# The order of wide and narrow matmul passes in a seven-product scheme, and one weight split earlier

## The chip, the core and the metric

The kernel runs on one core of one Trainium2 chip. The metric is device time in microseconds (us) from start to end of one execution; lower is better. On the core, TensorE (PE) multiplies a stationary block of 128x128 weights with a moving block of up to 512 columns and adds the result into a bank of PSUM (128 partitions x 512 floats). ScalarE (ACT), VectorE (DVE) and GpSimd (POOL) do element-wise work, SyncE (SP) issues most DMA transfers. Each engine works through its own list in order and waits on semaphores of the others.

## What is computed

A decoder trunk of two layers on 512 tokens of width 1024 (tokens are the columns, channels the partitions, 8 chunks of 128). Layer 0 mixes tokens by a gated linear recurrence and pooled differences, layer 1 by a convolution module; each then has cross-attention into 256 memory tokens and a gated feed-forward block (FFN) with a short convolution. The two parts that matter here:

```python
def conformer_conv(x, norm, w1, b1, dw_w, dw_b, ln_g, ln_b, w2, b2):
    h = rms_norm(x, norm) @ w1 + b1
    h = jax.nn.glu(h, axis=-1)
    h = causal_dwconv(h, dw_w, dw_b)
    h = jax.nn.silu(layer_norm(h, ln_g, ln_b))
    return h @ w2 + b2

def conv_ffn(x, norm, w_up, dw_w, dw_b, w_down):
    h = rms_norm(x, norm) @ w_up
    g = causal_dwconv(h[..., :D_FF], dw_w, dw_b)
    u = h[..., D_FF:]
    return (jax.nn.gelu(g) * u) @ w_down
```

with D_FF = 3072.

## The kernel before

**Split operands.** Every float32 operand is split into a high part (`hi`, rounded by a ScalarE copy) and a low part (`lo = x - hi`, a VectorE subtraction). A product is then high x high + high x low + low x high, three matmul passes for each 128 channels of the contraction (`mm3`, lines 187 to 192: L190, L191, L192 are the three passes). Weights come by DMA into a buffer `raw` (a ring of 3) and are split by `load_w` into `whi` and `wlo` (L170 on ScalarE, L171 on VectorE).

**Seven products.** The FFN's up projection computes two channel blocks (gate and value, 128 channels each) from two halves of the contraction and two halves of the tokens. It uses a scheme with seven block products instead of eight, with sums of weight blocks ("s1" to "s4") and sums of token halves (T1 to T4); "a11", "a12", "a22" are plain blocks. Each product runs over 4 chunks of 128 channels and 256 tokens. For channels 6 to 21 (`WIDE`) the high and the low part of the tokens lie side by side in one tile of 512 columns, so that a chunk takes two passes: a *wide* one of 512 columns (high weights times [high | low]) and a *narrow* one of 256 columns (low weights times high, added into the left half of the bank). `Seven.product` (line 812) writes them, L820 is the matmul:

```python
steps = [(ps, wh, x), (ps[:, :M], wl, x[:, :M])]
for i, (to, part, by) in enumerate(steps if c < 3 else steps[::-1]):
```

So one product is the series wide, narrow, wide, narrow, wide, narrow, narrow, wide. For the other channels a product takes the three passes of `mm3`, each of 256 columns.

**A unit.** `unit(c)` of `ffn` is one channel's turn. On TensorE, in a row: s1 (into the bank `stat`, called H), s2 (into F), a12 (into G), s3 (into F), then the down projection of an earlier channel (24 passes of 512 columns, `mm3`), then a11 of the next channel (`ahead`), s4 (into H) and a22 (into F). Between them ScalarE and VectorE empty the banks (L175, L958, L970 and others), split the weight blocks of the coming channel (L862 high, L869 low), and GpSimd's DMA queue forms the weight sums. The FFN and the attention stand in `manual_schedule` regions: there the program order of each engine is the order written in the code. `mm_ps()` gives the next bank of a pool of 5 (`mm`) or, at every few calls while `wide[0]` is set, of a pool of 2 (`aux`); `stat_ps()` gives the one bank `stat`.

**The end of the convolution module** (layer 1, lines 1750 to 1820). After the layer norm the eight chunks `outs[c]` are multiplied by the norm's scale (`scaled`, L1778, VectorE), passed through SiLU (`silu`, L1782, ScalarE) and split (L180 high, L185 low) to `xs[c]`. At the same time the memory values of layer 1 end: their sums (L468, TensorE) stand in the banks `ps[0]` and `ps[1]`, and `mem.scaled` takes them out (L474 on ScalarE, L478 on VectorE), which sets the banks free. The eight output projections `pw2` follow in the order `PAIRED` = 0, 4, 1, 5, ...: the first three together, chunk by chunk as `xs[c]` gets ready (`project_all`), the others one after the other (`project`). Behind the manual region a list scheduler orders the instructions.

Of the kernel before, what the change touches and what calls it, by code (L numbers as in the profile page):

```python
# [15 lines left out]
P = 128  # L16
T = 512
# [4 lines left out]
M = 256  # L22
# [8 lines left out]
PAIRED = (0, 4, 1, 5, 2, 6, 3, 7)  # L31
# [31 lines left out]
def trunk(ctx: ExitStack, tc: tile.TileContext, I: dict, out: list):  # L63
    nc = tc.nc
    V, A, G, PE = nc.vector, nc.scalar, nc.gpsimd, nc.tensor
# [14 lines left out]
    def nm(s):  # L80
        uid[0] += 1
        return f"{s}_{uid[0]}"
# [16 lines left out]
    def main_ps():  # L99
        return psum.tile([P, T], F32, tag="mm", name=nm("mm"))  # L100

    def aux_ps():
        return aux.tile([P, T], F32, tag="aux", name=nm("aux"))
# [3 lines left out]
    def mm_ps():  # L107

        wide[1] += 1
        return aux_ps() if wide[0] and wide[1] % 7 in (2, 5) else main_ps()  # L110

    def stat_ps():
        return stat.tile([P, T], F32, tag="stat", name=nm("stat"))
# [37 lines left out]
    def load_w(src=None, eng=None, raw=None, parts=1, ahead=AHEAD, park=False):  # L151

        with tc.high_priority(ahead):
            if raw is None:
                raw = wp.tile([P, D], F32, tag="raw", name=nm("raw"), bufs=3)
                fetched[0] = nc.sync.dma_start(raw, src)
            if park:
                both = [split(raw[:, i : i + T], None, None, eng) for i in (0, T)]
                return [b[0] for b in both], [b[1] for b in both]
            hi = wp.tile([P, D], F32R, tag="whi", name=nm("whi"))  # L160
            lo = wp.tile([P, D], F32R, tag="wlo", name=nm("wlo"))
            n = D // parts
            for i in range(0, D, n):
                split(raw[:, i : i + n], hi[:, i : i + n], lo[:, i : i + n], eng)
        return hi, lo

    def split(src, hi=None, lo=None, eng=None):
        hi = act_r() if hi is None else hi
        lo = act_r() if lo is None else lo
        A.activation(hi, src, AF.Copy)  # L170
        fetched[1] = (eng or V).tensor_tensor(lo, src, hi.bitcast(F32), op=ALU.subtract)  # L171
        return hi, lo
# [5 lines left out]
    def high(src, hi=None):  # L178
        hi = act_r() if hi is None else hi
        A.activation(hi, src, AF.Copy)  # L180
        return hi

    def low(src, hi, lo=None):
        lo = act_r() if lo is None else lo
        V.tensor_tensor(lo, src, hi.bitcast(F32), op=ALU.subtract)  # L185
        return hi, lo

    def mm3(ps, w, x, first, last, onto=False):
        (wh, wl), (xh, xl) = w, x
        PE.matmul(ps, wh, xh, start=first, stop=False, skip_group_check=onto)  # L190
        PE.matmul(ps, wh, xl, start=False, stop=False, skip_group_check=onto)  # L191
        return PE.matmul(ps, wl, xh, start=False, stop=last, skip_group_check=onto)  # L192
# [16 lines left out]
    def blk(w, i, n=P):  # L209
        hi, lo = (w.hi, w.lo) if isinstance(w, Piece) else w  # L210
        if isinstance(hi, list):
            hi, lo, i = hi[i // T], lo[i // T], i % T
        return hi[:, i : i + n], lo[:, i : i + n]
# [158 lines left out]
    def project_all(ws, xs, ps=None, at=0, last=True):  # L372

        ps = ps or [mm_ps() for _ in ws]
        for k, x in enumerate(xs, at):
            for w, p in zip(ws, ps):
                mm3(p, blk(w, k * P), x, k == 0, last and k == C - 1)
        return ps
# [361 lines left out]
    class Seven:  # L740
# [68 lines left out]
                    move(hi[:, M:], lo[:, :M])  # L809
            self.beside.add(j)  # L810

        def product(self, ps, w, j, first=True):

            for c in range(4):
                wh, wl = blk(w, c * P)
                if ps.shape[-1] == T:
                    x = self.both(j, c)
                    steps = [(ps, wh, x), (ps[:, :M], wl, x[:, :M])]
                    for i, (to, part, by) in enumerate(steps if c < 3 else steps[::-1]):
                        PE.matmul(  # L820
                            to, part, by, start=first and c == 0 and i == 0, stop=c == 3 and i == 1, skip_group_check=True
                        )
                else:
                    mm3(ps, (wh, wl), self.block(j, c), first and c == 0, c == 3, not first)
            return ps

    class Blocks:
# [51 lines left out]
    def pairs_of(layer):  # L879
        return {c: Blocks(I["wpair"][layer * (CF - PLAIN) + c - PLAIN]) for c in range(PLAIN, CF)}  # L880

    def ffn(layer, norm, nxt, seven, pairs):
# [105 lines left out]
            V.tensor_tensor(ys[c][1], y, ys[c][0].bitcast(F32), op=ALU.subtract)  # L988

        def m(c, ps, block, j, first=True):  # L990
            seven.product(ps, pairs[c].w[block], j, first)

        def ahead(c):

            G, F = bank(c), bank(c)
            m(c, G, "a11", seven.B11)
            if c == WIDE[0] + 1:
                PE.matmul(F, pairs[c].w["a11"][0][:, :P], seven.both(seven.B11, 0), start=True, stop=True)
            A.activation(F, G, AF.Copy)
            return G, F  # L1000

        def unit(c):
# [3 lines left out]
            down, seeded = downs.get(c), c > GC  # L1006
            H = stat_ps() if wide(c) else main_ps()[:, :M]
            m(c, H, "s1", seven.T1)
            if c <= second:
                high(c + 1, "s3")  # L1010
            next(left, None)
            if c <= second:
                low(c + 1, "s3")

            m(c, F, "s2", seven.T2, False)
            u, f, g = tmp_f(), tmp_f(), tmp_f()
            if wide(c):
# [167 lines left out]
        first, second = PLAIN, PLAIN + 1  # L1185
        done.update((first, name) for name in ("a11", "a22", "a12", "s3", "s1", "s2"))
        with tc.high_priority(AHEAD):
            w = [Piece(I["wup"][(layer * 2 + k) * PLAIN]) for k in range(2)]
# [9 lines left out]
        if nxt:  # L1198
# [10 lines left out]
            for j in range(C // 2):  # L1209
                for i in range(2):  # L1210
                    ps = mm_ps()
# [314 lines left out]
    def conformer(norm, nxt, mem, parked):  # L1526
# [136 lines left out]
        xs = [None] * C  # L1663
        mem.eng = G
        with tc.manual_schedule(engines=ORDERED | {mybir.EngineType.SP}):
            key2 = mem.products(parked[2], ks=range(4))
            ps0, (xh, xl) = [mm_ps(), mm_ps()], norm.x[0]
            first = [(p, blk(ws[k], 0)) for p, k in zip(ps0, ("G0", "V0"))]
# [56 lines left out]
            ps = [[mm_ps(), mm_ps()] for _ in range(2)]  # L1725
            mem.eng = None
            steps = (_ for h in range(2) for _ in mem.sums(h, ps[h], ready[4 * h :]))
# [24 lines left out]
            def halves(raw):  # L1752
                both = [split(raw[:, i : i + T]) for i in (0, T)]
                return [b[0] for b in both], [b[1] for b in both]

            pw = [halves(raws[0])]
# [19 lines left out]
            def scaled(c):  # L1776
                if c < C:
                    V.tensor_tensor(outs[c], outs[c], r, op=ALU.mult)  # L1778

            def silu(c):  # L1780
                if c < C:
                    A.activation(outs[c], outs[c], AF.Silu, scale=col("c_ln_g", c), bias=col("c_ln_b", c))  # L1782
# [4 lines left out]
            for c in range(C):  # L1787
                hi = high(outs[c])
                silu(c + 1)
                scaled(c + 2)  # L1790
                xs[c] = low(outs[c], hi)
                if c == 0:
                    mem.scaled(0, ps[0])
                elif c == 1:
                    pw.append(load_w(I["pw2"][PAIRED[2]]))
                elif c == 5:
                    mem.scaled(1, ps[1])
            mem.eng = None
# [3 lines left out]
        def finish(n, ps):  # L1802
            V.scalar_tensor_tensor(X[n], ps, col("c_b_pw2", n), X[n], op0=ALU.add, op1=ALU.add)
            nxt.feed(n)

        six = Seven(nxt, 3)
        for n, ps in zip(PAIRED, project_all(pw, xs)):
            finish(n, ps)
        for n in PAIRED[3:]:
            if n == 5:  # L1810
# [13 lines left out]
    with tc.manual_schedule(engines=ORDERED | {mybir.EngineType.SP}):  # L1824
# [20 lines left out]
        ps = [[mm_ps(), mm_ps()] for _ in range(2)]  # L1845
        steps = mem.sums(0, ps[0], ready)
# [19 lines left out]
        steps = mem.sums(1, ps[1], late)  # L1866
# [7 lines left out]
        w = [Piece(I["wk"][0])]  # L1874
# [55 lines left out]
    pairs = pairs_of(0)  # L1930
    mem, parked = ffn(0, n2, n3, attention(0, n1, mem, n2, six, pairs[PLAIN]), pairs)
    six = conformer(n3, n4, mem, parked)
    pairs = pairs_of(1)
    ffn(1, n5, None, attention(1, n4, mem, n5, six, pairs[PLAIN]), pairs)
# [78 lines left out]
```

## Time and profile before

| | us |
|---|---|
| median of 3 runs | 1421.2 (1420.17 to 1423.81) |
| the profiled execution | 1420.88 |
| its span, first to last instruction | 1419.1 |
| TensorE busy | 1408.8 |
| VectorE busy | 1139.4 |
| ScalarE busy | 938.0 |
| GpSimd busy | 318.1 |

The granted TensorE clock is 0.999 of full speed over the span. A row of the timeline reads: start, duration (both us from the span's start), engine, source line, operation, the tile written and the tiles read, partitions x columns, count of merged instructions, and in brackets the engine's idle time before it and what ended that. TensorE's matmuls are pipelined, so a row's duration overlaps the next row; the distance of two starts tells what a pass took. A row of the waits reads: who waited, for whom, us in total, times, the longest. In the rows of "order" below, which come from the program and have no times, a matmul reads bank<-moving operand,weights.

### The profile page before, as it was taken

How to read it: one execution, taken by the hardware profiler on the slowest of the kernel's cores; microseconds unless marked ns; L12 is line 12 of the kernel's file. 1: busy time of each engine (PE TensorE's matmuls, PEld its weight loads, DVE VectorE, ACT ScalarE, POOL GpSimd, SP SyncE). 2: the span in 40 equal slices, each digit the busy share in tenths (PEclk: the TensorE clock that was granted, in tenths of full speed). 3: DMA queues.
4: the chain of work that ended last, by engine and by line, in shares of the span. 5: the costliest groups of instructions: out<-in, count | busy, mean ns of one | idle time of the engine just before them, and what ended most of it. 6: DMA issues, size and time to landing. Idle time of an engine off the chain costs nothing.

```text
span 1419.1 us, 21330 instructions
## 1 busy us (share of the span) xinstructions
PE 1408.8 (99%) x7756; PEld 1214.8 (86%) x7756; DVE 1139.4 (80%) x1924; ACT 938.0 (66%) x1688; POOL 318.1 (22%) x333
## 2 busy tenths in 40 slices
PE   9999999999999999999999999999999999999998
PEld 7988888998898888888988777899889888888897
DVE  6987776778877888878799997968788788788775
ACT  7678744776567676676666547766756766766664
POOL 0011310110122222222008993011002222222211
PEclk9999999999999999999999999999999999999999
DMA  8623232544387777676433454345338776776751
GB/s 300 202 75 102 92 119 82 112 119 131 99 204 168 165 178 177 162 179 170 123 119 119 119 158 154 105 89 137 107 98 194 180 175 163 177 178 162 169 135 60
DMA packets 80026, 204.23 MB, mean 144 GB/s; under 512 B 9008, under 2 KB 9520, under 8 KB 79920
## 3 DMA queue, kind: packets, MB, share of 16 engines
q1 hardware_dynamic: 50688, 149.89, 32.7%
q0 software_dynamic: 28800, 52.44, 21.5%
q8 instruction: 61, 1.00, 0.3%
q10 hardware_dynamic: 432, 0.54, 0.1%
q14 instruction: 45, 0.37, 0.1%
HBM read 145.16 MB, written 2.10 MB: 104 GB/s over the span
## 4 chain that ended last, share of the span: by engine, by line
PE 92%; DVE 2%; ACT 2%; DMA 2%; issue 1%; POOL 0%; SPq 0%; ACTq 0%; DVEq 0%; POOLq 0%
PE mm L820 16%; PE mm L190 15%; PE mm L192 15%; PE mm L191 15%; PE aux L190 7%; PE aux L191 7%; PE aux L192 7%; PE stat L820 6%; PE mm L468 1%; PE mm L1571 1%; DVE wlo L171 1%; DMA raw<-in_wk 1%; DMA raw<-in_wv 1%; ACT whi L170 1%; PE aux L542 0%
## 5 line engine op out<-in xcount | busy, mean ns | idle before, releaser
L190 PE MATMUL mm<-act,whi 128*128 128x512 f32 (+2 forms) x803 | 295.8, 370 | 0.6 <-ACT whi L170 0.5
L191 PE MATMUL mm<-act,whi 128*128 128x512 f32 (+2 forms) x803 | 295.7, 368 | 0.1
L192 PE MATMUL mm<-act,wlo 128*128 128x512 f32 (+2 forms) x803 | 295.6, 368 | 0.0
L190 PEld LDWEIGHTS mm<-act,whi 128*128 128x128 f32 x803 | 151.1, 188 | 26.9 <-ACT whi L170 0.9
L191 PEld LDWEIGHTS mm<-act,whi 128*128 128x128 f32 x803 | 151.3, 188 | 25.5 <-DVE act L171 1.0
L192 PEld LDWEIGHTS mm<-act,wlo 128*128 128x128 f32 x803 | 151.3, 188 | 25.1 <-DVE wlo L171 0.6
L869 DVE TENSOR_TENSOR bigr<-raw,bigr 128x512 fp32r<-128x512 f32 x176 | 120.4, 686 | 64.0 <-ACT bigr L862 63.4
L862 ACT ACTIVATE bigr<-raw 128x512 fp32r<-128x512 f32 x176 | 109.4, 622 | 83.3 <-DVE wlo L207 80.8
L190 PE MATMUL aux<-act,whi 128*128 128x512 f32 x399 | 155.5, 390 | 0.0
L191 PE MATMUL aux<-act,whi 128*128 128x512 f32 x399 | 155.3, 389 | 0.0
L192 PE MATMUL aux<-act,wlo 128*128 128x512 f32 x399 | 155.2, 389 | 0.0
L875 POOL DMA_DIRECT2D raw<-wa x100 | 96.4, 983 | 254.1 <-DVE bigr L869 167.2
L820 PE MATMUL mm<-bigr,bigr 128*128 128x512 f32 (+1 forms) x768 | 150.9, 339 | 0.0
L170 ACT ACTIVATE whi<-raw 128x1024 fp32r<-128x1024 f32 (+1 forms) x95 | 96.5, 1020 | 81.9 <-PE mm L191 44.1
L820 PEld LDWEIGHTS mm<-bigr,bigr 128*128 128x128 f32 x768 | 124.4, 188 | 17.5
L872 POOL DMA_DIRECT2D raw<-raw x50 | 43.3, 866 | 385.8 <-DVE wlo L869 304.1
L171 DVE TENSOR_TENSOR wlo<-raw,whi 128x1024 fp32r<-128x1024 f32 (+1 forms) x75 | 90.2, 1210 | 18.2 <-ACT whi L170 17.9
L820 PE MATMUL mm<-act,whi 128*128 128x512 f32 x256 | 95.6, 397 | 0.0
L192 PEld LDWEIGHTS aux<-act,wlo 128*128 128x128 f32 x399 | 74.9, 188 | 15.8
L191 PEld LDWEIGHTS aux<-act,whi 128*128 128x128 f32 x399 | 75.0, 188 | 15.6
L877 POOL DMA_DIRECT2D raw<-wa x50 | 43.2, 864 | 200.3 <-DVE bigr L869 94.2
L190 PEld LDWEIGHTS aux<-act,whi 128*128 128x128 f32 x399 | 74.9, 188 | 14.1
(377 smaller groups left out, 3391.5 us busy)
## 6 DMA issues: line engine op xcount, KB each, us to landing
raw<-wa POOLq DMA_DIRECT2D x150, 256.0 KB, 3.9
wa<-in_wpair SPq DMA_DIRECT2D x88, 256.0 KB, 3.7
raw<-in_wpair SPq DMA_DIRECT2D x44, 512.0 KB, 4.0
big<-in_wdown SPq DMA_DIRECT2D x42, 512.0 KB, 4.6
raw<-raw POOLq DMA_DIRECT2D x50, 256.0 KB, 3.8
raw<-in_pw SPq DMA_DIRECT2D x24, 512.0 KB, 3.8
raw<-in_win SPq DMA_DIRECT2D x20, 512.0 KB, 3.5
raw<-in_wk SPq DMA_DIRECT2D x16, 512.0 KB, 3.6
```

The source lines that it names most:

```text
L170: A.activation(hi, src, AF.Copy)
L171: fetched[1] = (eng or V).tensor_tensor(lo, src, hi.bitcast(F32), op=ALU.subtract)
L190: PE.matmul(ps, wh, xh, start=first, stop=False, skip_group_check=onto)
L191: PE.matmul(ps, wh, xl, start=False, stop=False, skip_group_check=onto)
L192: return PE.matmul(ps, wl, xh, start=False, stop=last, skip_group_check=onto)
L468: PE.matmul(p, m[j], x, start=k == 0 and j == 0 and x is hi, stop=k == C - 1 and x is lo)
L820: PE.matmul(to, part, by, start=first and c == 0 and i == 0, stop=c == 3 and i == 1, skip_group_check=True)
L862: A.activation(self.w[name][0], self.block(name), AF.Copy)
L869: V.tensor_tensor(lo, self.block(name), hi.bitcast(F32), op=ALU.subtract)
L872: G.dma_start(self.r, self.z, accum_op=ALU.add)
L875: G.dma_start(block, self.a22, accum_op=ALU.add)
L877: G.dma_start(self.r, self.a12, accum_op=ALU.add)
```

## The change

In wide products the four wide passes stand together and the four narrow ones together. A product is *plain* (wide first) or *turned* (narrow first); turned are s4, a22, s2 and s3 in the FFN. At the end of the convolution module the load and split of the third `pw2` weight moves from the second turn of the loop over chunks to the first, and `mem.scaled(0)`, the values' scaling, from the first to the second; the third projection's bank is `stat` instead of the next of `mm_ps()`.

```diff
-        def product(self, ps, w, j, first=True):
-
-            for c in range(4):
-                wh, wl = blk(w, c * P)
-                if ps.shape[-1] == T:
-                    x = self.both(j, c)
-                    steps = [(ps, wh, x), (ps[:, :M], wl, x[:, :M])]
-                    for i, (to, part, by) in enumerate(steps if c < 3 else steps[::-1]):
-                        PE.matmul(
-                            to, part, by, start=first and c == 0 and i == 0, stop=c == 3 and i == 1, skip_group_check=True
-                        )
-                else:
-                    mm3(ps, (wh, wl), self.block(j, c), first and c == 0, c == 3, not first)
+        def product(self, ps, w, j, first=True, turned=False):
+
+            blocks = [(blk(w, c * P), self.both(j, c) if ps.shape[-1] == T else self.block(j, c)) for c in range(4)]
+            if ps.shape[-1] == T:
+                steps = [(ps, wh, x) for (wh, _), x in blocks], [(ps[:, :M], wl, x[:, :M]) for (_, wl), x in blocks]
+                steps = steps[1] + steps[0] if turned else steps[0] + steps[1]
+                for i, (to, part, x) in enumerate(steps):
+                    PE.matmul(to, part, x, start=first and i == 0, stop=i == 7, skip_group_check=True)
+            else:
+                for c, (part, x) in enumerate(blocks):
+                    mm3(ps, part, x, first and c == 0, c == 3, not first)
             return ps
...
         def m(c, ps, block, j, first=True):
-            seven.product(ps, pairs[c].w[block], j, first)
+            seven.product(ps, pairs[c].w[block], j, first, block in ("s4", "a22", "s2", "s3"))
...
                 if c == 0:
+                    pw.append(load_w(I["pw2"][PAIRED[2]]))
+                elif c == 1:
                     mem.scaled(0, ps[0])
-                elif c == 1:
-                    pw.append(load_w(I["pw2"][PAIRED[2]]))
                 elif c == 5:
                     mem.scaled(1, ps[1])
...
-        for n, ps in zip(PAIRED, project_all(pw, xs)):
+        for n, ps in zip(PAIRED, project_all(pw, xs, [mm_ps(), mm_ps(), stat_ps()])):
             finish(n, ps)
```

TensorE, the products s1 (bank `stat_4402`) and s2 (bank `mm_4359`) of the first wide channel of layer 0, before: s1 and the first two rows of s2.

```order
L820 MATMUL stat_4402<-bigr_3236,bigr_4350 128x512
L820 MATMUL stat_4402<-bigr_3236,bigr_4350 128x256
L820 MATMUL stat_4402<-bigr_3236,bigr_4350 128x512
L820 MATMUL stat_4402<-bigr_3236,bigr_4350 128x256
L820 MATMUL stat_4402<-bigr_3237,bigr_4350 128x512
L820 MATMUL stat_4402<-bigr_3237,bigr_4350 128x256 x2
L820 MATMUL stat_4402<-bigr_3237,bigr_4350 128x512
L820 MATMUL mm_4359<-bigr_3238,bigr_4353 128x512
L820 MATMUL mm_4359<-bigr_3238,bigr_4353 128x256
```

The same place after the change: s1, which is plain, and the whole of s2, which is turned.

```order
L819 MATMUL stat_4402<-bigr_3236,bigr_4350 128x512 x2
L819 MATMUL stat_4402<-bigr_3237,bigr_4350 128x512 x2
L819 MATMUL stat_4402<-bigr_3236,bigr_4350 128x256 x2
L819 MATMUL stat_4402<-bigr_3237,bigr_4350 128x256 x2
L819 MATMUL mm_4359<-bigr_3238,bigr_4353 128x256 x2
L819 MATMUL mm_4359<-bigr_3239,bigr_4353 128x256 x2
L819 MATMUL mm_4359<-bigr_3238,bigr_4353 128x512 x2
L819 MATMUL mm_4359<-bigr_3239,bigr_4353 128x512 x2
```

The same sixteen passes; the eight narrow ones of two products now stand in one row.

TensorE at the first three `pw2` projections, before. `mm_8965`, `mm_8966` and `mm_8967` are their banks; `act_8898` and `act_8902` are high and low part of chunk 0, `act_8908` and `act_8912` of chunk 1; `whi_8916` and `wlo_8917` are the third weight.

```order
L190 MATMUL mm_8965<-act_8898,act_8808 128x512
L191 MATMUL mm_8965<-act_8902,act_8808 128x512
L192 MATMUL mm_8965<-act_8898,act_8809 128x512
L190 MATMUL mm_8966<-act_8898,act_8854 128x512
L191 MATMUL mm_8966<-act_8902,act_8854 128x512
L192 MATMUL mm_8966<-act_8898,act_8855 128x512
L190 MATMUL mm_8965<-act_8908,act_8808 128x512
L190 MATMUL mm_8966<-act_8908,act_8854 128x512
L190 MATMUL mm_8967<-act_8898,whi_8916 128x512
L191 MATMUL mm_8967<-act_8902,whi_8916 128x512
L191 MATMUL mm_8965<-act_8912,act_8808 128x512
```

After: `whi_8906` and `wlo_8907` are the third weight, `stat_8967` its bank, `act_8910` and `act_8914` are chunk 1.

```order
L190 MATMUL mm_8965<-act_8898,act_8808 128x512
L191 MATMUL mm_8965<-act_8902,act_8808 128x512
L192 MATMUL mm_8965<-act_8898,act_8809 128x512
L190 MATMUL stat_8967<-act_8898,whi_8906 128x512
L191 MATMUL stat_8967<-act_8902,whi_8906 128x512
L190 MATMUL mm_8965<-act_8910,act_8808 128x512
L192 MATMUL stat_8967<-act_8898,wlo_8907 128x512
L190 MATMUL stat_8967<-act_8910,whi_8906 128x512
L191 MATMUL mm_8965<-act_8914,act_8808 128x512
L192 MATMUL mm_8965<-act_8910,act_8809 128x512
L191 MATMUL stat_8967<-act_8914,whi_8906 128x512
L192 MATMUL stat_8967<-act_8910,wlo_8907 128x512
```

The third projection has changed places with the second (`mm_8966`), whose passes on chunks 0 and 1 now follow as a block of six.

VectorE at the same place, before (`bigr<-mm` are the scaled values, `actf` the chunks):

```order
L1778 TENSOR_TENSOR actf_7910<-actf_7910,aux_8874 128x512
L185 TENSOR_TENSOR act_8902<-actf_7682,act_8898 128x512
L478 SCALAR_TENSOR_TENSOR bigr_7204<-mm_8702,rt,bigr_7203 128x512
L478 SCALAR_TENSOR_TENSOR bigr_7206<-mm_8703,rt,bigr_7205 128x512
L1778 TENSOR_TENSOR actf_8019<-actf_8019,aux_8874 128x512
L185 TENSOR_TENSOR act_8912<-actf_7779,act_8908 128x512
L171 TENSOR_TENSOR wlo_8917<-raw_8914,whi_8916 128x1024
```

And after:

```order
L1776 TENSOR_TENSOR actf_7910<-actf_7910,aux_8874 128x512
L185 TENSOR_TENSOR act_8902<-actf_7682,act_8898 128x512
L171 TENSOR_TENSOR wlo_8907<-raw_8904,whi_8906 128x1024
L1776 TENSOR_TENSOR actf_8019<-actf_8019,aux_8874 128x512
L185 TENSOR_TENSOR act_8914<-actf_7779,act_8910 128x512
L478 SCALAR_TENSOR_TENSOR bigr_7204<-mm_8702,rt,bigr_7203 128x512
L478 SCALAR_TENSOR_TENSOR bigr_7206<-mm_8703,rt,bigr_7205 128x512
```

The third weight's low half now stands ahead of chunk 1's low half, and the two steps that free the banks `mm_8702` and `mm_8703` behind it. ScalarE's list moves in the same way: `whi_8906` stands where the first two L474 stood.

## The prediction

> **What bounds the kernel now.** I read the page first, then the waits of TensorE, then the order of its passes in time.
>
> ```profile
> span 1419.1 us, 21330 instructions
> PE 1408.8 (99%) x7756; PEld 1214.8 (86%) x7756; DVE 1139.4 (80%) x1924; ACT 938.0 (66%) x1688; POOL 318.1 (22%) x333
> PE 92%; DVE 2%; ACT 2%; DMA 2%; issue 1%; POOL 0%; SPq 0%; ACTq 0%; DVEq 0%; POOLq 0%
> PE stat L143 <- POOL onesf L132: 1.0, 1, 1.0
> PE mm L468 <- ACT whi L170: 0.9, 1, 0.9
> PE mm L190 <- ACT whi L170: 0.5, 1, 0.5
> ```
>
> TensorE (PE) is busy 99% and carries 92% of the chain; its three longest waits are 1.0, 0.9 and 0.5 us. So the kernel ends when PE has started its last pass, and an edit is worth what it takes off the distances from one pass's start to the next. A matmul's row says it lasts 0.40 (512 columns) or 0.28 us (256), but the next one starts well before that end; only starts count. One product of the feed-forward blocks (a11 of one channel), and the start of the next:
>
> ```profile
> 601.45 0.40 PE L820 MATMUL mm<-act,whi 128*128 128x512 f32 x1
> 601.68 0.28 PE L820 MATMUL mm<-act,wlo 128*128 128x256 f32 x1
> 601.80 0.40 PE L820 MATMUL mm<-act,whi 128*128 128x512 f32 x1
> 602.03 0.28 PE L820 MATMUL mm<-act,wlo 128*128 128x256 f32 x1
> 602.15 0.40 PE L820 MATMUL mm<-act,whi 128*128 128x512 f32 x1
> 602.39 0.40 PE L820 MATMUL mm<-act,wlo 128*128 128x256 f32 x2
> 602.63 0.40 PE L820 MATMUL mm<-act,whi 128*128 128x512 f32 x1
> 602.87 1.58 PE L820 MATMUL mm<-bigr,bigr 128*128 128x512 f32 x8
> ```
>
> Four wide passes (W) and four narrow ones (N) take 602.87 - 601.45 = 1.42 us. What they would take without changes of width is read where many of one kind stand together, in the cross-attention: 24 wide, 24 narrow, 24 wide.
>
> ```profile
> 307.19 0.28 PE L190 MATMUL aux<-bigr,act 128*128 128x256 f32 x1
> ...
> 307.42 0.28 PE L192 MATMUL aux<-bigr,act 128*128 128x256 f32 x1
> ...
> 309.94 0.28 PE L192 MATMUL aux<-bigr,act 128*128 128x256 f32 x1
> 310.06 0.40 PE L190 MATMUL mm<-act,whi 128*128 128x512 f32 x1
> ...
> 311.22 0.39 PE L192 MATMUL mm<-act,wlo 128*128 128x512 f32 x1
> ...
> 315.30 0.39 PE L192 MATMUL mm<-act,wlo 128*128 128x512 f32 x1
> ```
>
> Settled: 18 wide starts from 311.22 to 315.30, 0.2267 us each; 21 narrow ones from 307.42 to 309.94, 0.120 each. At a turn they differ. The first five wide passes after narrow ones take 311.22 - 310.06 = 1.16 instead of 5 x 0.2267 = 1.133: 0.027 lost. The first two narrow ones after wide ones take 0.23 instead of 0.24 (0.008 less at the trace's full resolution, nearly all in the first). So one round trip between long runs costs about 0.019 us. After only four wide passes it is less:
>
> ```profile
> 735.86 0.40 PE L1670 MATMUL mm<-act,whi 128*128 128x512 f32 x1
> ...
> 736.79 0.28 PE L190 MATMUL mm<-bigr,act 128*128 128x256 f32 x1
> ...
> 737.50 0.28 PE L190 MATMUL mm<-bigr,act 128*128 128x256 f32 x1
> ```
>
> Four wide passes take 0.93 (0.907 settled, 0.023 lost), the six narrow ones behind them 0.71 (0.72 settled, 0.010 won back): 0.012 for this round trip.
>
> **Part 1, the order inside a product.** It adds and removes no instruction; it moves passes inside a product, on PE alone. The place is one channel's unit: seven products and 24 wide passes of the down projection. It returns every
>
> ```profile
> 456.53 0.39 PE L820 MATMUL mm<-act,whi 128*128 128x512 f32 x1
> ...
> 655.62 0.39 PE L820 MATMUL mm<-act,whi 128*128 128x512 f32 x1
> ```
>
> (655.62 - 456.53) / 13 units = 15.315 us. Settled, the unit would take 52 x 0.2267 + 28 x 0.120 = 11.788 + 3.360 = 15.148. So changes of width cost 0.167 us now, over 21 round trips (three in each W N W N W N N W): 0.008 each, short runs being the cheaper ones.
>
> After: a11 plain, s4 and a22 turned, s1 plain, s2 turned, a12 plain, s3 turned, then down. The runs of a unit are 8 N (a11, s4), 4 W (s4), 4 N, 8 W (a22, s1), 8 N, 8 W (s2, a12), 8 N and 32 W (s3, down, next a11). Four round trips: three whose wide run has five passes or more, 0.019 each, one with four, 0.012: 0.069. Gain 0.167 - 0.069 = 0.098 us a unit. Wide units are 16 channels in each of 2 layers: 32 x 0.098 = **3.1 us**. Bounds: nothing, if the distances belong to these operands and not to the turns; 32 x 0.167 = 5.3 us, if a turn cost nothing at all.
>
> The Trainium skill (TensorE: Matmul & The Clock Gate, Back-to-back issue gap) gives the distance of isolated warm matmuls as columns / 2.4 + 2.5 ns, whatever stands before: an estimate by it is 0.216 and 0.109 us, 1.30 us for a product in every order, so by that rule this part is worth nothing. The trace has 0.227, 0.120 and 1.42, so the rule's sizes do not hold in this stream; its indifference to order is the first rival.
>
> Can the new order make PE wait? A turned product needs its low weights at its start instead of one pass (0.23 us) later, and everything behind it comes 0.014 us a product sooner (0.098 / 7). The nearest deadlines of a unit:
>
> ```profile
> 612.75 0.88 DVE L175 TENSOR_TENSOR tmp<-stat,tmp 128x256 f32<-128x256 f32 x2 [0.19 <-PE stat L820]
> 613.55 0.68 DVE L869 TENSOR_TENSOR bigr<-raw,bigr 128x512 fp32r<-128x512 f32 x1
> 613.96 1.55 PE L820 MATMUL stat<-bigr,bigr 128*128 128x512 f32 x8
> 615.35 1.56 PE L820 MATMUL mm<-bigr,bigr 128*128 128x512 f32 x8
> ```
>
> The low half of s2's weights is done at 614.23, its product starts at 615.35: 1.1 us to spare. The bank of s4 is read until 613.63, and s1 writes it from 613.96: 0.33 us to spare. Both cover the shift.
>
> **Part 2, the third pw2 weight ahead of the scaled values.** The rows around the wait of 0.5 us:
>
> ```profile
> 878.31 0.81 ACT L1782 ACTIVATE actf<-actf,par 128x512 f32<-128x512 f32 x1
> 879.02 1.25 ACT L474 ACTIVATE bigr<-mm,rt 128x512 fp32r<-128x512 f32 x2
> 879.72 1.41 DVE L478 SCALAR_TENSOR_TENSOR bigr<-mm,rt,bigr 128x512 fp32r<-128x512 f32 x2 [0.59 <-ACT bigr L474]
> 879.84 0.39 PE L190 MATMUL mm<-act,act 128*128 128x512 f32 x1
> 881.05 0.68 DVE L1778 TENSOR_TENSOR actf<-actf,aux 128x512 f32<-128x512 f32 x1
> 881.39 1.05 ACT L170 ACTIVATE whi<-raw 128x1024 fp32r<-128x1024 f32 x1
> 881.64 0.69 DVE L185 TENSOR_TENSOR act<-actf,act 128x512 fp32r<-128x512 f32 x1
> 882.47 1.22 DVE L171 TENSOR_TENSOR wlo<-raw,whi 128x1024 fp32r<-128x1024 f32 x1
> 882.49 0.50 PE L190 MATMUL mm<-act,whi 128*128 128x512 f32 x1 [0.51 <-ACT whi L170]
> 884.89 0.61 PE L190 MATMUL mm<-act,act 128*128 128x512 f32 x2
> ```
>
> The first two contraction steps are 18 passes, 4.08 us settled; PE takes 884.89 - 879.84 = 5.05, so 0.97 is lost. In the new order ScalarE splits the third weight where L474 stood: 879.02 + 1.05 = 880.07, early enough. But VectorE now waits for that, then does its low half (1.22), one scaled tile (0.68) and the low half of the second operand (0.69): 882.66. PE has eight passes until then (1.81 us) and waits with four more of these steps that need that operand or stand behind it, to 883.57; only then come the six passes of the second product, whose bank L478 frees at 882.66 + 0.70 = 883.36. Step two ends at 883.57 + 6 x 0.227 = 884.93 against 884.89. The wait moves from the weight to the second operand, so I take **0.0 us**; the ends are -0.97 (all of it gone) and +0.3 (the pass behind the old wait lasts 0.50 instead of 0.39; three such starts behind new waits). The scaled values, now later by 2 us, feed nothing on PE but that bank. The weight's transfer keeps its place in SP's queue, nothing of POOL's moves, and the raw buffer is freed sooner. The later projections swap banks and four passes of the fourth product move forward; the cover is PE's own unbroken work from 884.89 on.
>
> **Sum**: 3.1 + 0.0 = 3.1 us off 1420.9, the profiled execution's time (span 1419.1 and 1.8 around it). The median of the runs shown, 1421.2, lies 0.3 above it: 1418.1, faster by 0.22%. About 0.3% (4.3 us) is what a measurement of this kernel can tell from no change.
>
> **Rivals.**
> 1. The order is free: the 0.167 us belong to these operands, not to the turns. For it: a wide pass in these products takes 0.23 to 0.24 beside narrow ones on both sides. Against it: passes of other operands show the same 0.23 behind a turn and 0.2267 six passes later. Time 1421.2.
> 2. More is gained. If a round trip stays at the 0.008 that short runs pay now, a unit keeps 4 x 0.008 = 0.032 and 32 x 0.135 = 4.3 us go: 1416.9. If VectorE reaches the second operand in time as well, 0.97 more: 1415.9; that alone, beside the 3.1, gives 1417.1. For it: the run of four costs less than long ones. Against it: three of the four new wide runs are long enough for the full 0.027.
> 3. Slower: s1 waits for s4's bank. VectorE runs its list in order, and if another step ahead of the two sums of s4 becomes late by d, PE waits d - 0.33 in each of 32 units. It eats the gain from d = 0.43 and passes 0.3% slower from 0.33 + 7.4 / 32 = 0.56; at d = 0.6 the time is 1418.1 + 32 x 0.27 = 1426.7. Against it: VectorE's order in the units is the same, and PE does not come sooner by more than 0.014 a product.
>
> **How the numbers follow.** My forecast has 0.60, rival 1 0.14, rival 2 0.21, rival 3 0.05. The time is the forecast's, 1418.1; the range goes up to nearly no change, 1420.9, and down into rival 2, 1416.4. What is left out is the far part of rival 2 (0.07), the upper half of rival 1 (0.08) and rival 3. Faster by over 0.3% needs 1416.9 or less: half of rival 2 and a tail of the forecast, 0.16. Slower by over 0.3% is rival 3's upper part, 0.03. Within: 0.81.
>
> **What the next profile would show.** Right: a unit of 15.22 us; seven products and their neighbours with narrow passes at 0.120 in a row (0.113 for the first) and wide ones at 0.233, 0.236, 0.229, then 0.227; no new wait of PE in the units; near 882 us a wait of PE for VectorE's low half (L185) or the bank (L478) in place of the one for ScalarE's weight, and the third contraction step some 5.05 us after the first start. Wrong: a unit of 15.3 with wide passes above 0.232 to the end of a run (rival 1), one of 15.18 or a step two that ends 4.1 us after its start (rival 2), or a row of waits before s1 for VectorE (rival 3).

## The result, and the profile after

The changed kernel takes 1418.4 us (median of 18 runs, 1418.0 to 1420.4), the kernel before 1420.9 (18 runs): ratio 0.9982, 95% interval 0.9975 to 0.9990. By the ratio that is 2.6 us less (0.18%), by the medians 2.4; 3.1 us (0.22%) were forecast, and the time lies inside the range of 1416.4 to 1420.9. From the page of the changed kernel's profile, with its three longest waits of TensorE:

```profile
span 1416.3 us, 21327 instructions
PE 1406.7 (99%) x7756; PEld 1215.3 (86%) x7756; DVE 1139.4 (80%) x1924; ACT 937.6 (66%) x1688; POOL 317.6 (22%) x333
PE 94%; DVE 2%; ACT 2%; DMA 1%; issue 0%; POOL 0%; ACTq 0%; POOLq 0%; DVEq 0%; SPq 0%
PE stat L143 <- POOL onesf L132: 1.0, 1, 1.0
PE stat L324 <- DVE tmp L258: 0.5, 1, 0.5
PE mm L191 <- DVE act L185: 0.5, 1, 0.5
```

TensorE still sets the end; among its waits the one for ScalarE's weight (L170, at the projections) is gone and one for VectorE's low half (L185) has come. The unit, from the first a11 of the thirteen to the last:

```profile
455.45 0.39 PE L819 MATMUL mm<-act,whi 128*128 128x512 f32 x1
...
653.49 0.39 PE L819 MATMUL mm<-act,whi 128*128 128x512 f32 x1
```

(653.49 - 455.45) / 13 = 15.234 us, against 15.315 before and 15.217 forecast. Inside one unit, the timeline of TensorE alone (rows of one tile are merged, x4 or x8, so that a product's start stands ahead of each):

```profile
607.80 1.07 PE L819 MATMUL mm<-act,whi 128*128 128x512 f32 x4
608.71 0.64 PE L819 MATMUL mm<-act,wlo 128*128 128x256 f32 x4
609.18 1.57 PE L819 MATMUL stat<-act,bigr 128*128 128x256 f32 x8
610.59 1.56 PE L819 MATMUL mm<-bigr,bigr 128*128 128x256 f32 x8
611.99 1.56 PE L819 MATMUL stat<-bigr,bigr 128*128 128x512 f32 x8
613.39 1.56 PE L819 MATMUL mm<-bigr,bigr 128*128 128x256 f32 x8
614.79 1.07 PE L819 MATMUL mm<-act,whi 128*128 128x512 f32 x4
```

a11 takes 609.18 - 607.80 = 1.38 us (1.387 is the settled sum of four wide and four narrow passes): its wide passes follow the down projection and its narrow ones take 0.47. s4, a22, s1 and s2 take 1.41, 1.40, 1.40 and 1.40. The mean over a unit's seven products, with 24 x 0.2267 = 5.44 for the down projection, is (15.234 - 5.44) / 7 = 1.399; before it was (15.315 - 5.44) / 7 = 1.411.

The end of the convolution module, chosen rows of ScalarE, VectorE and TensorE:

```profile
877.16 1.04 ACT L170 ACTIVATE whi<-raw 128x1024 fp32r<-128x1024 f32 x1
877.98 0.39 PE L190 MATMUL mm<-act,act 128*128 128x512 f32 x1
878.23 1.23 DVE L171 TENSOR_TENSOR wlo<-raw,whi 128x1024 fp32r<-128x1024 f32 x1 [0.96 <-ACT whi L170]
879.38 0.68 DVE L1776 TENSOR_TENSOR actf<-actf,aux 128x512 f32<-128x512 f32 x1
879.52 0.50 PE L192 MATMUL stat<-act,wlo 128*128 128x512 f32 x1
879.98 0.68 DVE L185 TENSOR_TENSOR act<-actf,act 128x512 fp32r<-128x512 f32 x1
880.58 1.40 DVE L478 SCALAR_TENSOR_TENSOR bigr<-mm,rt,bigr 128x512 fp32r<-128x512 f32 x2
880.72 0.50 PE L191 MATMUL mm<-act,act 128*128 128x512 f32 x1 [0.46 <-DVE act L185]
883.13 0.39 PE L190 MATMUL mm<-act,act 128*128 128x512 f32 x1
```

The weight's high half comes early (878.20), but VectorE has idled 0.96 us for it. So its low half ends at 879.46, and TensorE's pass on it starts at 879.52; chunk 1's low half ends at 880.66, and TensorE, which waits 0.46 us for it, goes on at 880.72. The first 18 passes take 883.13 - 877.98 = 5.15 us, 0.10 more than before.

Not all of the span's 2.8 us (1419.1 to 1416.3) belongs to the change. The first wide product starts at 424.69 us in the changed kernel's profile and at 425.62 in that of the kernel before, which is 0.93 of it. No instruction ahead of that point is changed, and over the ten profiles of this study (before, after and eight experiments) that start lies anywhere from 424.61 to 425.93. So below the unit and the 18 passes, which repeat within 0.015 us between profiles of one order, carry the verdicts, and the timed ratio is held against them.

### The profile page after: what moved, and what is told of

Its sections match the earlier page's. It is cut to its first block, busy times and chain, and to the rows that moved or that the text cites. A ratio compares the mean times of both kernels' runs of the same rounds, so it can differ in the third digit from the quotient of the medians.

```text
span 1416.3 us, 21327 instructions
## 1 busy us (share of the span) xinstructions
PE 1406.7 (99%) x7756; PEld 1215.3 (86%) x7756; DVE 1139.4 (80%) x1924; ACT 937.6 (66%) x1688; POOL 317.6 (22%) x333
## 4 chain that ended last, share of the span: by engine, by line
PE 94%; DVE 2%; ACT 2%; DMA 1%; issue 0%; POOL 0%; ACTq 0%; POOLq 0%; DVEq 0%; SPq 0%
PE mm L819 16%; PE mm L190 15%; PE mm L191 15%; PE mm L192 15%; PE aux L190 7%; PE aux L192 7%; PE aux L191 7%; PE stat L819 6%; PE mm L468 2%; PE mm L1569 1%; DVE wlo L171 1%; PE aux L542 0%; ACT whi L170 0%; PE aux L468 0%; POOL tmp L1416 0%
## 5 line engine op out<-in xcount | busy, mean ns | idle before, releaser
L191 PE MATMUL mm<-act,whi 128*128 128x512 f32 (+2 forms) x795 | 292.6, 368 | 0.1
L190 PE MATMUL mm<-act,whi 128*128 128x512 f32 (+2 forms) x795 | 292.6, 369 | 0.0
L192 PE MATMUL mm<-act,wlo 128*128 128x512 f32 (+2 forms) x795 | 292.4, 368 | 0.0
L191 PEld LDWEIGHTS mm<-act,whi 128*128 128x128 f32 x795 | 149.9, 188 | 25.2 <-DVE act L171 1.0
L191 PE MATMUL aux<-act,whi 128*128 128x512 f32 x399 | 155.3, 389 | 0.0
L170 ACT ACTIVATE whi<-raw 128x1024 fp32r<-128x1024 f32 (+1 forms) x95 | 96.3, 1019 | 82.4 <-PE mm L191 44.6
L819 PE MATMUL mm<-bigr,bigr 128*128 128x256 f32 (+1 forms) x768 | 150.6, 338 | 0.0
L819 PEld LDWEIGHTS mm<-bigr,bigr 128*128 128x128 f32 x768 | 113.6, 189 | 11.4
L171 DVE TENSOR_TENSOR wlo<-raw,whi 128x1024 fp32r<-128x1024 f32 (+1 forms) x75 | 90.3, 1210 | 19.1 <-ACT whi L170 18.9
L191 PEld LDWEIGHTS aux<-act,whi 128*128 128x128 f32 x399 | 75.0, 188 | 15.5
L1604 DVE SCALAR_TENSOR_TENSOR aux<-h,par,aux 128x491 f32<-128x491 f32 (+18 forms) x120 | 81.3, 732 | 0.6
```

Source lines behind the costliest of these rows:

```text
L819: PE.matmul(to, part, x, start=first and i == 0, stop=i == 7, skip_group_check=True)
L1604: V.scalar_tensor_tensor(ps[:, s:], h[:, : T - s], tap(s, c), ps[:, s:], op0=ALU.mult, op1=ALU.add)
```

## The experiments

**The two parts alone.** e1 has the joined passes and the old end of the convolution module; e2 the new end and the old passes.

```diff
 # e1, against the changed kernel
                 if c == 0:
+                    mem.scaled(0, ps[0])
+                elif c == 1:
                     pw.append(load_w(I["pw2"][PAIRED[2]]))
-                elif c == 1:
-                    mem.scaled(0, ps[0])
...
-        for n, ps in zip(PAIRED, project_all(pw, xs, [mm_ps(), mm_ps(), stat_ps()])):
+        for n, ps in zip(PAIRED, project_all(pw, xs)):
```

> Joined passes as in the changed kernel, the end of the convolution module as before. If the two parts stand alone: a unit of 15.234 us as in the changed kernel (15.315 before), the first 18 passes of the pw2 projections 5.05 us as before, in all 2.4 us (two FFNs, 1.26 and 1.10 in the profiles) less than before. Rival (the order of passes is free, the gain came from elsewhere): units of 15.315 and no gain.

> The third pw2 weight ahead of the scaled values alone, passes as before. My theory (the wait only moves to VectorE's low half): units 15.315, the first 18 passes 5.15 us against 5.05, time 0.0 to 0.2 us above before. Rival (the wait of 0.5 us goes): 18 passes in 4.1 to 4.5 us, 0.5 to 1.0 us below before.

e1: ratio to before 0.9986 (0.9977 to 0.9995). TensorE, the unit's first and last start and the first and nineteenth pass of the projections:

```profile
455.43 0.39 PE L819 MATMUL mm<-act,whi 128*128 128x512 f32 x1
...
653.56 0.39 PE L819 MATMUL mm<-act,whi 128*128 128x512 f32 x1
...
877.83 0.39 PE L190 MATMUL mm<-act,act 128*128 128x512 f32 x1
...
882.88 0.39 PE L190 MATMUL mm<-act,act 128*128 128x512 f32 x1
```

Unit 198.13 / 13 = 15.241, 18 passes 5.05. e2: ratio 1.0000 (0.9992 to 1.0009).

```profile
455.56 0.39 PE L820 MATMUL mm<-act,whi 128*128 128x512 f32 x1
...
654.46 0.39 PE L820 MATMUL mm<-act,whi 128*128 128x512 f32 x1
...
878.85 0.39 PE L190 MATMUL mm<-act,act 128*128 128x512 f32 x1
...
883.99 0.39 PE L190 MATMUL mm<-act,act 128*128 128x512 f32 x1
```

Unit 198.90 / 13 = 15.300, 18 passes 5.14. The whole gain is the order of the passes; the weight's new place gains nothing and costs 0.1 us that no timing resolves.

**How many round trips of width, and how long the runs.** e3 never turns a product (seven round trips a unit, of four wide and four narrow passes but for the long run of the down projection), e4 is the kernel before without the reversed last chunk (28 round trips of one and one).

```diff
 # e3, against the changed kernel
-                steps = steps[1] + steps[0] if turned else steps[0] + steps[1]
+                steps = steps[0] + steps[1]
 # e4, against the kernel before
-                    for i, (to, part, by) in enumerate(steps if c < 3 else steps[::-1]):
+                    for i, (to, part, by) in enumerate(steps):
```

> As the changed kernel, but all products plain (wide first), so seven round trips of width a unit instead of four, each of four wide and four narrow passes. By the profile of the changed kernel four wide passes behind narrow ones lose 0.023 and the four narrow ones behind them win back 0.009: 7 x 0.014 is about 0.10 and the unit 15.25. Rival (every round trip costs the 0.0215 that a trip of the changed kernel costs on average): 7 x 0.0215 = 0.15, unit 15.30. Rival (order is free): 15.315.

> As the kernel before, but the last chunk is not reversed: wide, narrow, wide, narrow, four times, in every product, 28 round trips a unit. Theory of round trips (0.008 each, as the 21 before): 0.22, unit 15.37, 1.8 us slower than before. Rival (a wide pass beside a narrow one costs nothing: 0.233 + 0.113 is the settled 0.347, and only two of a kind in a row behind a turn lose): unit 15.15 to 15.18, 4 to 5 us faster than before. Order is free: 15.315.

e3: ratio 0.9992 (0.9984 to 1.0001), unit (654.88 - 456.41) / 13 = 15.267. e4: ratio 1.0015 (1.0006 to 1.0024), unit (655.63 - 456.12) / 13 = 15.347. Their rows of TensorE, e3 then e4:

```profile
456.41 0.39 PE L819 MATMUL mm<-act,whi 128*128 128x512 f32 x1
...
654.88 0.39 PE L819 MATMUL mm<-act,whi 128*128 128x512 f32 x1
```

```profile
456.12 0.39 PE L820 MATMUL mm<-act,whi 128*128 128x512 f32 x1
...
655.63 0.39 PE L820 MATMUL mm<-act,whi 128*128 128x512 f32 x1
```

The same passes on the same operands take four different times, in the order that the round trips give, so the order is not free. That a pair of a wide and a narrow pass costs nothing (the rival of e4) falls too. The sizes were forecast less well: e3 lies between its forecast (15.25) and the rival of an equal price for every trip (15.30), e4 between a free order (15.315) and its forecast (15.37). Over the settled 15.148 the unit loses 0.199 with 28 trips (0.007 each), 0.167 with 21 (0.008), 0.119 with 7 (0.017) and 0.086 with the change's 4 (0.0215): fewer trips gain, but less than in proportion, since a trip between runs of four costs more than twice what one between single passes costs.

**The dear place among the four trips.** e7 leaves a22 plain, so that the runs are 8, 8, 4, 4, 8, 8, 8, 32 instead of 8, 4, 4, 8, 8, 8, 8, 32.

```diff
-            seven.product(ps, pairs[c].w[block], j, first, block in ("s4", "a22", "s2", "s3"))
+            seven.product(ps, pairs[c].w[block], j, first, block in ("s4", "s2", "s3"))
```

> The changed kernel, but a22 is plain: runs of 8 narrow, 8 wide, 4 narrow, 4 wide, 8 narrow, 8 wide, 8 narrow, 32 wide: again four round trips. Theory (what a trip costs hangs on the runs: the dear place of the changed kernel is the eight wide passes behind 4 wide and 4 narrow, which lose 0.045): 3 x 0.019 and one of 0.012, unit 15.217, 0.5 us below the changed kernel. Rival (any four trips cost the same 0.086): 15.234.

Ratio 0.9979 (0.9971 to 0.9988). Rows of e7: the unit's first and last start, and between them a22 and s1 of one unit:

```profile
456.67 0.39 PE L819 MATMUL mm<-act,whi 128*128 128x512 f32 x1
...
611.60 1.55 PE L819 MATMUL mm<-bigr,bigr 128*128 128x512 f32 x8
612.98 1.56 PE L819 MATMUL stat<-bigr,bigr 128*128 128x512 f32 x8
614.38 1.56 PE L819 MATMUL mm<-bigr,bigr 128*128 128x256 f32 x8
...
654.45 0.39 PE L819 MATMUL mm<-act,whi 128*128 128x512 f32 x1
```

Unit 197.78 / 13 = 15.214; a22 takes 1.38 instead of 1.40, a22 and s1 together 2.78 instead of 2.80. With the same number of trips 0.020 us a unit are won, and the forecast of 15.217 holds. Its reason is not shown by this, since the edit changes a second thing. TensorE with its weight loads (PEld) at the start of s1, first in the changed kernel (a22's last pass and s1's first load), then in e7 (the load alone):

```profile
611.77 0.39 PE L819 MATMUL mm<-bigr,bigr 128*128 128x512 f32 x1
611.79 0.39 PEld L819 LDWEIGHTS stat<-bigr,bigr 128*128 128x128 f32 x2
```

```profile
612.86 0.31 PEld L819 LDWEIGHTS stat<-bigr,bigr 128*128 128x128 f32 x2
```

At the trace's full resolution s1's first load starts 0.023 to 0.030 us behind the start of a22's last pass in 30 units of the changed kernel, and always 0.115 to 0.117 us after VectorE has read s4's bank (0.116 in e6, where TensorE waits for it outright): it is held for that bank. In e7, where a22 ends with narrow passes, it starts 0.002 to 0.003 us behind. The load is held in the kernel before, e1, e2 and e5 too, and not in e3, e4 and e8. Where it is held, units of one order differ (15.293 to 15.334 before, 15.226 to 15.247 after the change); where it is not, 26 units agree within 0.001. So how much of the 0.020 is due to the order of the runs, and how much to the held load, stays open: the eight wide passes of a22 and s1 lose 0.045 in the changed kernel, 0.024 of it in the first three, ahead of the held load. What the order does by itself is told by e4, e3 and e7, where the load is not held: 15.347, 15.267 and 15.214.

**A bank's deadline against a turn.** e6 puts the narrow passes of s4 and a22 together, then their wide ones: three trips, but s4 ends later. `joined`, which is new, writes the narrow passes of both products and then the wide ones of both; its body is left out here.

```diff
-            m(c, H, "s4", seven.B22, False)
-            m(c, F, "a22", seven.T4, False)
+            if wide(c):
+                seven.joined([(H, pairs[c].w["s4"], seven.B22), (F, pairs[c].w["a22"], seven.T4)])
+            else:
+                m(c, H, "s4", seven.B22, False)
+                m(c, F, "a22", seven.T4, False)
```

> The changed kernel, but the narrow passes of s4 and a22 stand together and then their wide ones: three round trips a unit instead of four, and s4 ends 0.48 us (four narrow passes) later against the next s1. If only turns count: unit 15.234 - 0.02 = 15.21. Rival (the bank deadline, my third rival: s4's bank is read until 0.31 us before s1 writes it): PE waits 0.17 us or a little more before s1 in every unit, unit 15.38 to 15.48, 4.5 to 8 us slower than the changed kernel.

Ratio 1.0060 (1.0046 to 1.0074), unit (659.50 - 456.56) / 13 = 15.611: slower by 0.38 a unit, more than forecast. The waits, and VectorE and TensorE around one s1:

```profile
PE stat L819 <- ACT x L914: 4.4, 28, 0.2
PE stat L819 <- DVE tmp L175: 0.3, 2, 0.2
615.94 1.07 PE L832 MATMUL mm<-bigr,bigr 128*128 128x512 f32 x4
616.14 0.88 DVE L175 TENSOR_TENSOR tmp<-stat,tmp 128x256 f32<-128x256 f32 x2 [0.61 <-PE stat L832]
617.17 1.16 PE L819 MATMUL stat<-bigr,bigr 128*128 128x512 f32 x4 [0.16 <-ACT x L914]
```

VectorE's two sums of H end at 617.02 and s1 starts at 617.17, 1.23 us after a22's wide passes began, which take 0.91 settled: 0.32 lost, and the four passes from that start last 1.16 instead of 1.07. (The row names ScalarE's L914 as the releaser. But in all 30 units in which s1 waits, s1 starts 0.146 or 0.147 us after the end of VectorE's second sum, whether L914 ends 0.08 or 0.32 us ahead of s1: it is VectorE, which reads s1's bank, that s1 waits for.) In the changed kernel the sums end at 611.67 and s1 starts at 611.99:

```profile
610.79 0.88 DVE L175 TENSOR_TENSOR tmp<-stat,tmp 128x256 f32<-128x256 f32 x2
611.99 1.56 PE L819 MATMUL stat<-bigr,bigr 128*128 128x512 f32 x8
```

So of the 0.32 us between them 0.15 are needed, and the true margin is 0.17: 0.48 - 0.17 is 0.31, what s1 is late by. Even that margin is not free: as the loads of e7 show, s1's first weight load is already held by 0.02 to 0.03 us in the kernel before and in the changed one, though no row of the waits says so.

**The weight's high half earlier still.** e5 takes it where ScalarE idles, ahead of the first SiLU.

```diff
+            third = Piece(I["pw2"][PAIRED[2]])
+            third.high()
             scaled(0)
             silu(0)
...
-                    pw.append(load_w(I["pw2"][PAIRED[2]]))
+                    third.low()
+                    pw.append(third)
```

> The changed kernel, with the high half of the third pw2 weight (ScalarE) taken ahead of the first SiLU, where ScalarE idles 1.44 us; its low half (VectorE) stays where the change put it. The scheduler also pulls the high half of the fourth weight ahead of the first SiLU, which starts some 0.4 us later. Theory (the wait moved because VectorE stood 0.96 us idle for that high half, and chunk 1's low half with it): VectorE goes on at once, PE's wait for chunk 1's low half shrinks from 0.46 to about 0.2, the first 18 passes take 4.3 to 4.6 us instead of 5.15, time 0.6 to 0.8 below the changed kernel. Rival (the second product's bank, set free by L478, is the limit): still 5.0 or more.

Ratio 0.9977 (0.9969 to 0.9986), 1417.5 us.

```profile
877.80 1.22 DVE L207 TENSOR_TENSOR wlo<-raw,whi 128x1024 fp32r<-128x1024 f32 x1
878.23 0.39 PE L190 MATMUL mm<-act,act 128*128 128x512 f32 x1
...
880.27 0.50 PE L191 MATMUL mm<-act,act 128*128 128x512 f32 x1
...
882.67 0.39 PE L190 MATMUL mm<-act,act 128*128 128x512 f32 x1
```

VectorE's L207 starts behind its neighbour with no idle time; 18 passes take 4.44, 0.71 less than in the changed kernel. The bank that L478 frees was not the limit, VectorE's idling was. The passes settled would take 4.08; TensorE still starts chunk 1's low half 0.23 late (880.27, eight passes after 878.23, instead of 878.23 + 8 x 0.2267 = 880.04).

**Both, the best version.**

> a22 plain and the third weight's high half earlier: unit 15.217 and 18 passes in 4.3 to 4.6 us, together 1.1 to 1.3 us below the changed kernel and 3 to 4 below the kernel before. Rival: none of both, as the changed kernel.

1417.0 us, ratio 0.9975 (0.9967 to 0.9984) to before. Unit and 18 passes:

```profile
455.35 0.39 PE L819 MATMUL mm<-act,whi 128*128 128x512 f32 x1
...
653.12 0.39 PE L819 MATMUL mm<-act,whi 128*128 128x512 f32 x1
...
877.49 0.39 PE L190 MATMUL mm<-act,act 128*128 128x512 f32 x1
...
881.93 0.39 PE L190 MATMUL mm<-act,act 128*128 128x512 f32 x1
```

15.213 and 4.44: both stages add, and it is the lowest median of all that ran. Its intervals overlap those of e5, e7 and the changed kernel; that it is faster than those is carried by the two stages, not by the timing.

## Why the prediction was right, point by point

- *What bounds the kernel*: TensorE's starts, right. The share of the chain is 94%, and the stages' gains are found again in the time. From the first to the last start of the products, the two FFNs take 249.32 and 249.14 us before and 248.06 and 248.06 after: 2.3 us less, and 0.1 more at the projections, 2.2 in all. The medians differ by 2.4, and the ratio's interval holds 1.4 to 3.6.
- *Part 1*: the mechanism is right (e1, e3, e4). The term was mis-sized: a unit keeps 0.086 us at its turns, not 0.069, and gains 0.081, not 0.098. Over all 32 units 2.3 us are gained instead of 3.1, 0.073 a unit, in part because the 13 units read before are slower than those of layer 1 (15.315 against 15.306). The step that was off is "three whose wide run has five passes or more, 0.019 each, one with four, 0.012". At full resolution the four trips cost 0.016 (the run of four), 0.036 (four narrow, then a22 and s1), 0.015 and 0.020. So nearly all of the miss is the one trip of a22 and s1, which stands behind only four narrow passes and in which s1's weight load is held; the prices came from runs that a long run stood ahead of, and in which nothing was held. e7, which takes away both, has 15.214, the forecast's 15.217. The sign "0.233, 0.236, 0.229, then 0.227" ends too early as well: a fourth and a fifth pass take 0.2325 and 0.231.
- *Part 2*: "the wait moves from the weight to the second operand" is what the rows of L171 (0.96 idle) and L191 (0.46) show, and e5 shows that VectorE's idling made it. Taken as 0.0, measured +0.10 (5.15 against 5.05, and 5.14 against 5.05 in e2 and e1): between the value taken and the upper end of +0.3. There are two new waits, not one: the pass on the weight's low half (879.52) is late as well, and each start behind such a wait comes some 0.1 us late.
- *The cover*: "0.33 us to spare" for H was too much. e6 shows that 0.15 of it is needed between VectorE's end and TensorE's start, and s1's weight load already stands behind VectorE in both kernels. The shift of some 0.01 us brought no new wait of a pass; what the held load costs a unit is not known.
- *Rival 1* (the order is free) falls by e3 and e4. The formula of the Trainium skill for isolated warm matmuls (TensorE: Matmul & The Clock Gate, Back-to-back issue gap), which takes a pass's columns alone, does not describe this stream: the same passes take 15.347, 15.315, 15.267 and 15.234 us. *Rival 2*: a trip between single passes is cheap (0.007), but the change's runs are not that short; its other half, VectorE in time, needed e5. *Rival 3* did not come; the place is real, as e6 shows.

## What to carry to other kernels

Where TensorE never idles, read the distance from start to start, for long runs of one shape and at each change of shape; the difference is a price that an order can lower, and its forecast needs rows with runs of the same lengths on both sides. Before a weight is split earlier, look at which engine's list it enters: a step that waits there holds what stands behind it, and the high half alone may be taken where the other engine idles. Ahead of moving a product's end, subtract from the margin the time that the writer needs behind the reader's end, and look at the writer's weight load as well as at its first pass.

## What the runs showed of the hardware that was not expected

A change of width between passes costs by the runs around it: 0.007 us a round trip at one and one (e4), 0.017 at four and four (e3), 0.0165 at runs of four to thirty-two (0.066 / 4 in e7). The changed kernel's 0.0215 (0.086 / 4) holds the trip with the held weight load. None of the runs here shows which part of TensorE makes the price; it stays open.

A bank that another engine still reads can hold the next product's weight load, with no wait of a pass in the profile: 0.02 to 0.03 us in each unit of the kernel before and of the changed one. And with that hold the units of one order stop being alike, by up to 0.04 us (15.293 to 15.334 before). Why they differ is not shown.
